# Dilated 3x3 convolution on one core: 960 one-element memsets on GpSimd, thirty in each of 32 groups

## The chip, the cores and the metric

The kernel runs on one core of one Trainium2 chip. The metric is the device time of one execution in microseconds. Most executions of a kernel agree within 0.3%. Engine names are those of the profile: PE is TensorE (PEld its weight loads), DVE is VectorE, ACT is ScalarE, POOL is GpSimd, SP is SyncE. A "q" behind a name (SPq, POOLq) is the engine's sequencer.

## The reference

Sixteen images of 64 channels and 64 x 64 pixels are convolved with 128 filters of 3 x 3, with dilation 2 and padding 2, in float32:

```python
batch, c_in, h, w, c_out, k, dilation = 16, 64, 64, 64, 128, 3, 2
...
x_pad = np.pad(x, ((0, 0), (0, 0), (pad, pad), (pad, pad)), mode='constant')
...
output[b, co] += weight[co, ci, kh, kw] * x_pad[b, ci, kh*dilation:kh*dilation+h, kw*dilation:kw*dilation+w]
```

Input x is 16.8 MB, the output 33.6 MB.

## The kernel before

Two images lie on the 128 partitions at once (64 channels each), so there are eight pairs. Each image has 64 rows, worked through in groups of 16 rows, four to a pair: 32 groups in all, and one loop over them.

SyncE loads the pairs as float32 (`load`, L65) and ScalarE casts them to float16 (`cast`, L74). VectorE adds rows two apart (`rowsum`, L86). TensorE makes three accumulations of a group in PSUM (`product`, L172): psP from the row sums, psA and psB from the cast rows. ScalarE copies psP to p_sb in SBUF (L234), and VectorE adds it to psA and to psB into the output tile osb (L241). SyncE stores the output tiles (L186, L192). Loads and stores share SyncE's one queue, in the order in which the code issues them.

Ahead of the loop stands the preparation of the weights: they are loaded (L89), VectorE, ScalarE and GpSimd form five combinations of filter rows (L112 to L116, GpSimd those at L113 and L116), and TensorE turns them. GpSimd also fills four small constants at the start of the program and makes the identity matrix (masks.py:197 and 199). It has no part in the loop.

The schedule is written by hand: the instructions of each engine keep the order of the code. The framework adds the semaphore waits that the tiles' reads and writes ask for. After the kernel's last instruction all engines meet in a closing exchange of semaphores (L310 in the profile).

The tile pools: wpool holds what lives for the whole kernel (weights, identity); the others rotate buffers.

Of the kernel before, what the change touches and what calls it, by code (L numbers as in the profile page):

```python
# [10 lines left out]
def kernel(  # L11
# [7 lines left out]
    nc = tc.nc  # L19
# [9 lines left out]
    P = 128  # L29
    f32 = mybir.dt.float32  # L30
# [14 lines left out]
    wpool = ctx.enter_context(tc.tile_pool(name="wpool", bufs=1))  # L45
# [15 lines left out]
    def load(pb, cuts=(0, H)):  # L61
        if pb not in x32_tiles:
            x32_tiles[pb] = fpool.tile([P, HW], f32, tag="x32", name="x32")
        for lo, hi in zip(cuts[:-1], cuts[1:]):
            nc.sync.dma_start(  # L65
                out=x32_tiles[pb][:, lo * W : hi * W], in_=x_pair[pb, :, lo * W : hi * W]
            )
# [10 lines left out]
    def rowsum(c):  # L78
        pb, g = divmod(c, NG)
        if g == 0:  # L80
            xs_tiles[pb] = sxpool.tile([P, HW // 2], f16, tag="xs", name="xs")
        v = x16_tiles[pb][:, g * GR * W : (g + 1) * GR * W].rearrange(
            "p (b e q) -> p b e q", e=2, q=2 * W
        )
        s = xs_tiles[pb][:, g * NH : (g + 1) * NH].rearrange("p (b q) -> p b q", q=2 * W)
        nc.vector.tensor_tensor(out=s, in0=v[:, :, 0], in1=v[:, :, 1], op=add)  # L86
# [67 lines left out]
    def casts(G):  # L154
        for n in range(2 if G else 3):
            c = ahead[0]
            if c >= ngroups or c > G + (7 if c < 2 * NG else 5):
                return
            cast(c)
            ahead[0] += 1  # L160

    def product(ps, src, kind, blk0, nblk, first, last):
        for j in (1, 0, 2):
            dw = (j - 1) * d
            o0, o1 = max(0, -dw), W - max(0, dw)
            t = kind * KW + j
            for hb in range(2):
                pp = slice(hb * CI, (hb + 1) * CI)
                rhs = src(pp, dw + o0, dw + o1)
                po = ps[:, hb * NH + blk0 * 2 * W : hb * NH + (blk0 + nblk) * 2 * W]  # L170
                po = po.rearrange("p (r w) -> p r w", w=W)[:, :, o0:o1]
                nc.tensor.matmul(  # L172
                    out=po,
                    lhsT=w_sb[pp, t * CO : (t + 1) * CO],
                    rhs=rhs,
                    start=first and j == 1,
                    stop=last and j == 2,
                )

    def blocks(x16, b0, n, e):  # L180
        v = x16.rearrange("p (b e r w) -> p b e r w", e=2, r=2, w=W)
        return lambda pp, c0, c1: v[pp, b0 : b0 + n, e, :, c0:c1]

    def store(pb, m, r0=0, r1=H, rows=((0, P),)):
        for lo, hi in rows:
            nc.sync.dma_start(  # L186
                out=out_img[2 * pb + m, lo:hi, r0 * W : r1 * W],
                in_=o_tiles[pb][lo:hi, m * HW + r0 * W : m * HW + r1 * W],
            )

    def store_both(pb, r0, r1):
        nc.sync.dma_start(  # L192
            out=out_img[2 * pb : 2 * pb + 2, :, r0 * W : r1 * W].rearrange("m o q -> o m q"),
            in_=o_tiles[pb].rearrange("p (m q) -> p m q", m=2)[:, :, r0 * W : r1 * W],
        )

    FOUR = ((0, P - 4), (P - 4, P))
    ROWS4 = 8

    for G in range(ngroups):  # L200
        pb, g = divmod(G, NG)
        x16 = x16_tiles[pb]
        xs = xs_tiles[pb].rearrange("p (r w) -> p r w", w=W)
        if g == 0:
            o_tiles[pb] = opool.tile([P, 2 * HW], f32, tag="osb", name="osb")
        o = o_tiles[pb].rearrange("p (m b e q) -> p m b e q", m=2, e=2, q=2 * W)
        b0 = g * NBLK

        def summed():
            ps = ppool.tile([P, 2 * NH], f32, tag="p", name="psP")  # L210
            sv = lambda pp, c0, c1: xs[pp, g * GR // 2 : (g + 1) * GR // 2, c0:c1]
            product(ps, sv, 0, 0, NBLK, True, True)
            return ps

        if G:
            psP = summed()

        psA = apool.tile([P, 2 * NH], f32, tag="ab", name="psA")
        product(psA, blocks(x16, b0, NBLK, 1), 1, 0, NBLK, True, False)
        z = 1 if g == 0 else 0  # L220
        product(psA, blocks(x16, b0 + z - 1, NBLK - z, 1), 2, z, NBLK - z, False, True)

        psB = apool.tile([P, 2 * NH], f32, tag="ab", name="psB")
        product(psB, blocks(x16, b0, NBLK, 0), 3, 0, NBLK, True, False)
        z = 1 if g == NG - 1 else 0
        product(psB, blocks(x16, b0 + 1, NBLK - z, 0), 4, 0, NBLK - z, False, True)

        if not G:
            psP = summed()

        if not G:
            casts(0)
        p_sb = spool.tile([P, 2 * NH], f32, tag="psb", name="p_sb")
        nc.scalar.copy(out=p_sb, in_=psP)  # L234
        if G:
            casts(G)
        if G + 1 < ngroups:
            rowsum(G + 1)
        pv = p_sb.rearrange("p (m b q) -> p m b q", m=2, q=2 * W)
        for e, ps in ((0, psA), (1, psB)):  # L240
            nc.vector.tensor_tensor(  # L241
                out=o[:, :, b0 : b0 + NBLK, e],
                in0=ps.rearrange("p (m b q) -> p m b q", m=2, q=2 * W),
                in1=pv,
                op=add,
            )

        if G == 0:
            load(XF, (0, H // 2))
        if pb == 0:  # L250
            if g % 2 == 1:
                store_both(0, (g - 1) * GR, (g + 1) * GR)
                if g == 1:
                    load(XF, (H // 2, H))
                else:
                    load(XF + 1)
        elif g == NG - 1 and pb == 1:
            store(1, 0)
            store(1, 1, 0, H // 2)
            load(XF + 2)  # L260
            store(1, 1, H // 2, H)
        elif g == NG - 1 and pb == 2:
            store(2, 0)
            load(XF + 3)
            store(2, 1)
            load(XF + 4)
        elif pb == npairs - 1:
            if g % 2 == 1:
                store(pb, 0, (g - 1) * GR, (g + 1) * GR)
                if g == 1:  # L270
                    store(pb, 1, 0, 2 * GR - ROWS4)
                    store(pb, 1, 2 * GR - ROWS4, 2 * GR, FOUR)
                else:
                    store(pb, 1, (g - 1) * GR, (g + 1) * GR)
        elif g == NG - 1:
            store(pb, 0)
            store(pb, 1)
# [37 lines left out]
```

## Time and profile before

| what | before |
|---|---|
| median of 3 runs | 126.81 us (126.58 to 126.98) |
| profiled execution, span from first to last instruction | 125.0 us |
| PE busy | 105.8 us (85%) |
| DVE busy | 91.0 us (73%), 103 instructions |
| ACT busy | 64.9 us (52%) |
| POOL busy | 2.2 us (2%), 8 instructions |
| DMA | 50.78 MB, mean 406 GB/s |

The profiled execution is told by its span alone, 125.0 us; the median of the runs is 1.8 us longer, which is what lies around the span. Busy time of an engine is the union of its instructions' recorded durations. A timeline line gives the start in us, the duration in us, the engine, the line of the code, the operation, output and input, and in brackets the engine's idle time before it with what ended it. A line "x4: 17/17/17, 124.3 to 124.9" gives a count, the shortest, median and longest duration in ns, and the first and last start in us.

### The profile page before, as it was taken

The page shows a single profiled execution, that of the slowest core. Times are in us where ns is not written, and L with a number is a line of the kernel's source. Part 1 is how long each engine was busy: PE and PEld are TensorE (multiplying, and loading weights), DVE is VectorE, ACT ScalarE, POOL GpSimd, SP SyncE. Part 2 cuts the span into 40 slices and gives each one's busy share as a digit, 9 for nine tenths or more (in the row PEclk, how much of TensorE's full clock was granted, in tenths as well). Part 3 has the DMA queues.
Part 4 walks back from the last instruction along what each step waited for, and adds up shares of the span by engine and source line. Part 5 has one row for each costly group of instructions (what it writes and reads, how often), then busy time and mean ns, then how long its engine had stood idle before and what let it go on. Part 6 is the DMA issues. An engine that isn't in the chain of part 4 may idle for free.

```text
span 125.0 us, 2343 instructions
## 1 busy us (share of the span) xinstructions
PE 105.8 (85%) x1002; PEld 57.0 (46%) x1002; DVE 91.0 (73%) x103; ACT 64.9 (52%) x68; POOL 2.2 (2%) x8
## 2 busy tenths in 40 slices
PE   6996999999999999999999999999999999600000
PEld 2353555555555555555555555555555555200000
DVE  0561998988898889888988898889888988700000
ACT  4188896665666566656665666566653333100000
POOL 2400000000000000000000000000000000000000
PEclk9999999999999999999999999999999999985555
DMA  5999999999999999999999999999999999999991
GB/s 142 368 450 435 430 401 315 430 422 420 443 427 435 412 441 438 401 435 435 425 430 427 420 435 430 435 420 435 420 430 430 430 425 435 430 414 412 420 395 73
DMA packets 4722, 50.78 MB, mean 406 GB/s; under 512 B 488, under 2 KB 488, under 8 KB 1000
## 3 DMA queue, kind: packets, MB, share of 16 engines
q1 hardware_dynamic: 4712, 50.63, 96.7%
q8 instruction: 8, 0.13, 0.4%
q14 instruction: 2, 0.02, 0.0%
HBM read 17.07 MB, written 33.55 MB: 405 GB/s over the span
## 4 chain that ended last, share of the span: by engine, by line
PE 76%; DMA 6%; ACT 2%; DVE 1%; DVEq 1%; SPq 1%; issue 0%
PE psA L172 31%; PE psB L172 30%; PE psP L172 16%; DMA x<-in_x_dram 6%; ACT x L74 2%; DVE osb L241 1%; DVEq L310 1%; ACT p_sb L234 1%; SPq L65 0%; SPq L89 0%; DVEq L241 0%
## 5 line engine op out<-in xcount | busy, mean ns | idle before, releaser
L172 PEld LDWEIGHTS <-w_sb 64*128 64x128 f16 x960 | 54.6, 94 | 45.8 <-issue 1.4
L234 ACT COPY p_sb<-psP 128x1024 f32<-128x1024 f32 x32 | 32.4, 1012 | 36.9 <-issue 21.5
L241 DVE TENSOR_TENSOR osb<-psA,p_sb 128x1024 f32<-128x1024 f32 x32 | 39.2, 1225 | 13.4 <-PE psA L172 9.8
L172 PE MATMUL psA<-x,w_sb 64*128 64x496 f16 (+3 forms) x384 | 45.1, 365 | 0.0
L172 PE MATMUL psB<-x,w_sb 64*128 64x496 f16 (+3 forms) x384 | 45.1, 365 | 0.0
L241 DVE TENSOR_TENSOR osb<-psB,p_sb 128x1024 f32<-128x1024 f32 x32 | 39.1, 1222 | 0.0
L74 ACT CAST x<-x 128x1024 f16<-128x1024 f32 (+2 forms) x31 | 32.1, 1044 | 0.5 <-DMA x<-in_x_dram 0.3
L172 PE MATMUL psP<-xs,w_sb 64*128 64x496 f16 (+1 forms) x192 | 26.0, 371 | 1.1 <-ACT p_sb L234 1.1
L86 DVE TENSOR_TENSOR xs<-x 128x512 f16<-128x512 f16 x32 | 13.3, 416 | 0.4 <-ACT x L74 0.4
L102 PE MATMUL dm<-zero 128*128 128x512 f16 x12 | 5.3, 579 | 1.2 <-DVE zero L94 1.2
L102 PEld LDWEIGHTS <-zero 128*128 128x128 f16 x12 | 1.4, 128 | 3.2 <-issue 1.8
L112 DVE CAST wd<-w 128x192 f16<-128x192 f32 x1 | 0.5, 503 | 2.4 <-DMA w<-in_weight_dram 2.4
L125 PEld LDWEIGHTS <-wd 128*64 128x64 f16 x30 | 1.0, 118 | 1.8 <-DVE wd L112 0.8
L137 ACT CAST w_sb<-wt 128x384 f16<-128x384 f32 x1 | 0.5, 478 | 2.3 <-PE wt L125 2.3
L114 ACT ACT_TABLE_LOAD x1 | 1.3, 1283 | 0.7 <-PEq L296 0.7
L125 PE MATMUL wt<-ident,wd 128*64 128x128 f16 x30 | 1.6, 241 | 0.0
L114 ACT CAST wd<-w 128x192 f16<-128x192 f32 x1 | 0.5, 539 | 1.5 <-DMA w<-in_weight_dram 1.5
L139 DVE CAST w_sb<-wt 128x384 f16<-128x384 f32 x1 | 0.6, 557 | 0.7 <-PE wt L125 0.7
L135 DVE CAST w_sb<-wt 128x384 f16<-128x384 f32 x1 | 0.6, 558 | 0.5 <-PE wt L125 0.5
L94 DVE MEMSET zero<- 128x256 uint32 x1 | 0.3, 272 | 0.9 <-PEq L296 0.9
L113 POOL TENSOR_TENSOR wd<-w 128x192 f16<-128x192 f32 x1 | 0.8, 799 | 2.3 <-DMA w<-in_weight_dram 2.3
L116 POOL CAST wd<-w 128x192 f16<-128x192 f32 x1 | 0.8, 806 | 0.0
(11 smaller groups left out, 3.8 us busy)
## 6 DMA issues: line engine op xcount, KB each, us to landing
out_dram<-osb SPq DMA_DIRECT2D x13, 2048.0 KB, 14.9
x<-in_x_dram SPq DMA_DIRECT2D x6, 2048.0 KB, 17.0
out_dram<-osb SPq DMA_DIRECT2D x5, 1024.0 KB, 13.1
x<-in_x_dram SPq DMA_DIRECT2D x2, 1024.0 KB, 13.2
x<-in_x_dram SPq DMA_DIRECT2D x1, 1088.0 KB, 5.6
x<-in_x_dram SPq DMA_DIRECT2D x1, 960.0 KB, 7.4
out_dram<-osb SPq DMA_DIRECT2D x1, 768.0 KB, 15.4
w<-in_weight_dram SPq DMA_DIRECT2D x1, 288.0 KB, 2.8
```

Source lines behind the costliest of these rows:

```text
L74: nc.scalar.copy(out=x16_tiles[pb][:, lo * W : hi * W], in_=x32_tiles[pb][:, lo * W : hi * W])
L86: nc.vector.tensor_tensor(out=s, in0=v[:, :, 0], in1=v[:, :, 1], op=add)
L102: nc.tensor.matmul(out=dm[:, 0:512], lhsT=zero[:, 0:P], rhs=zero)
L113: nc.gpsimd.tensor_tensor(out=wdv[:, 3], in0=wv[:, 0], in1=wv[:, 1], op=sub)
L114: nc.scalar.copy(out=wdv[:, 2], in_=wv[:, 0])
L116: nc.gpsimd.tensor_copy(out=wdv[:, 4], in_=wv[:, 2])
L125: nc.tensor.matmul(out=wts[k % 3][r * CI : (r + 1) * CI, c0 + j * CO : c0 + (j + 1) * CO], lhsT=wd[:, t * CI : (t + 1) * CI], rhs=ident,)
L135: nc.vector.tensor_copy(out=t0[0], in_=t0[1])
L172: nc.tensor.matmul(out=po, lhsT=w_sb[pp, t * CO : (t + 1) * CO], rhs=rhs, start=first and j == 1, stop=last and j == 2,)
L234: nc.scalar.copy(out=p_sb, in_=psP)
L241: nc.vector.tensor_tensor(out=o[:, :, b0 : b0 + NBLK, e], in0=ps.rearrange("p (m b q) -> p m b q", m=2, q=2 * W), in1=pv, op=add,)
L310: with _tile.TileContext(nc) as tc:
```

## The change

A tile of one float32 on each partition is taken from the pool of lasting tiles, and in each of the 32 groups, behind VectorE's two additions and ahead of the group's loads and stores, GpSimd is given thirty memsets of the tile's first partition, one element each. No instruction reads the tile.

```diff
@@ -194,6 +194,8 @@
+    tick = wpool.tile([P, 1], f32, name="tick")
+
     FOUR = ((0, P - 4), (P - 4, P))
     ROWS4 = 8
@@ -245,6 +247,8 @@
                 op=add,
             )
 
+        for _ in range(30):
+            nc.gpsimd.memset(tick[0:1], 0.0)
         if G == 0:
             load(XF, (0, H // 2))
         if pb == 0:
```

## The prediction

> **What bounds the kernel now.** I read the page's busy row and its forty slices, then the stretches, then GpSimd's own timeline, and last the program's closing line. The slices:
>
> ```profile
> PE   6996999999999999999999999999999999600000
> ...
> DMA  5999999999999999999999999999999999999991
> ```
>
> TensorE stops after about 108 us, but the DMA row stays at 9 to the last slice but one. The stretches (us, then busy time and count of PE, PEld, DVE, ACT, POOL, then granted clock, DMA share, GB/s) show the same with numbers:
>
> ```profile
> 36.00:67.00 31.00, 31.00 (x304) 17.02 (x300) 27.37 (x31) 19.64 (x21) 0.00 (x0) 1.00 1.00 425
> 108.00:124.00 16.00, 0.11 (x2) 0.00 (x0) 1.46 (x2) 0.00 (x0) 0.00 (x0) 0.61 0.89 373
> ```
>
> The DMA share is 1.00 while TensorE works, and 16 us of stores are still to drain after the last matmul. So the 50.78 MB set the end: the compute engines run ahead of the queue, and the chain that names TensorE for 76% of the span ends in the output drain. GpSimd is idle, 0.00 us busy, in every stretch after 5.2 us. All that it does is this:
>
> ```profile
> 0.24 0.10 POOL L296 MEMSET const-float32-0.0<- 128x1 f32 x1 [0.24 <-issue]
> 0.27 0.10 POOL L296 MEMSET const-float32-1.0<- 128x1 f32 x1
> 0.31 0.10 POOL L296 MEMSET const-bfloat16-1.0<- 128x1 bf16 x1
> 0.34 0.10 POOL L296 MEMSET const-uint8-127<- 128x1 uint8 x1
> 0.73 0.20 POOL masks.py:197 MEMSET ident<- 128x128 f16 x1 [0.29 <-POOLq L296]
> 1.01 0.29 POOL masks.py:199 TENSOR_SCALAR_AFFINE_SELECT ident<-ident 128x128 f16<-128x128 f16 x1
> 3.59 0.80 POOL L113 TENSOR_TENSOR wd<-w 128x192 f16<-128x192 f32 x1 [2.29 <-DMA w<-in_weight_dram]
> 4.33 0.81 POOL L116 CAST wd<-w 128x192 f16<-128x192 f32 x1
> ```
>
> Its last result, the cast, is done at 4.33 + 0.81 = 5.14 us. After that it only stands in the program's closing exchange of semaphores (first and last start in us):
>
> ```profile
> L310 POOLq EVENT_SEMAPHORE  x4: 17/17/17, 124.3 to 124.9; - x4
> L310 SPq DRAIN  x3: 7/7/7, 124.2 to 124.5; - x3
> ```
>
> GpSimd gathers the other engines there, at 124.3 us, and the span ends at 125.0. Whoever comes last to that exchange sets the end; today it is SyncE, with the last store landed.
>
> **The change, part by part.** Nothing is removed. The order of instructions on TensorE, VectorE, ScalarE and SyncE is the same in both programs; only buffer numbers and line numbers differ. GpSimd gets 960 memsets between its cast (L116) and the closing line. Nothing of another engine stands in their waits, so the place in the groups' loop holds nothing back: GpSimd runs through all 960 from 5.14 us on.
>
> What the words of the change hide is in the built program. All 960 memsets write the same element of the one tile tick, and from the second on each carries a wait on GpSimd's own completion semaphore, one count higher each time: memset k may start only when memset k-1 has finished writing. The four const memsets above carry no such wait, and start 0.10 / 3 = 33 ns apart although each takes 99 to 102 ns. At that pace the 960 would cost 32 us and be over at 37. With the waits they cannot overlap, and the period is the memset's own time plus the way from its end to the start of the next. A period p puts GpSimd's end at 5.14 + 960 p; it arrives at the closing exchange after SyncE if p is over (124.3 - 5.14) / 960 = 124 ns. This 124 ns decides the case.
>
> - Own time: 99 ns, from the const f32 memsets (128 partitions by one element). A memset of a single partition is nowhere in the trace; these are the nearest rows, and I take their time for it. The 128-element ident memset at 204 ns fits a fixed part near 98 plus 0.83 ns an element.
> - Gap after it: the one instruction on GpSimd that waits for GpSimd's own semaphore is the affine select at masks.py:199, which waits for the ident memset. It starts at 1.01, the memset ends at 0.73 + 0.204 = 0.934: 76 ns. That is the upper bound from rows, since a configuration instruction stands between the two in the program, and since the select must read, where a memset need not. The lower bound is the tightest wait elsewhere: p_sb is ready at 10.93 + 1.01 = 11.94 and VectorE's L241 starts at 11.97, 30 ns. A gap of nothing, or a negative one (a gain), is excluded by what the wait says: the count must rise before the next may begin.
>
> So p is between 99 + 30 = 129 and 99 + 76 = 175 ns, and both lie over 124. I put two thirds of the weight on the row of the same engine, the same semaphore and the same kind of predecessor: 129 + 2/3 x 46 = 160 ns. That GpSimd is slow to act on a wait is seen at the weights too: on the same landing VectorE and ScalarE start at 3.54 and GpSimd at 3.59.
>
> The sum: 960 x 0.160 = 153.6 us, from 5.14 on, so the memsets end at 158.7. Behind the last one stand a drain and the closing exchange, from 124.3 to 125.0 in the trace, 0.7 us, with 0.1 us for the drain: the span becomes 159.5. The profiled span of before is 125.0 and the median of its runs 126.81, so 1.8 us lie around the span: 161.3 us. With 129 ns it is 5.14 + 123.8 + 0.8 + 1.8 = 131.5, with 175 ns 5.14 + 168.0 + 2.6 = 175.7. Of the 960, the first 745 (119.2 / 0.160) lie beside the stores and cost nothing; the other 215 stick out past the end.
>
> Two small parts more. Instructions have to be fetched: the page's queue q8 shows 8 packets and 0.13 MB, 16 KB each. For the 2343 instructions of the trace that is 0.13 MB / 2343 = 55 bytes each, so 960 more are an estimated 0.053 MB, 0.1% of 50.78 MB, or 0.13 us of a saturated DMA. The 34 us by which the memsets outlast the stores cover it; without that cover, in the first rival below, it costs those 0.13 us. And VectorE shares the SBUF with GpSimd: its busy time is 91.0 of 125.0, and it waits 9.8 us for TensorE at L241, so small delays fall into slack, and larger ones are below the memsets' end as well.
>
> **The rivals.** First, hidden after all, not slower: the wait is resolved while the write of the one before is still on its way to memory (the 99 ns of a record may be mostly the acknowledgement, and the next memset's start may lie inside it), and the period is under 124 ns. For it: the const memsets have three in flight at once, 33 ns apart; L116 starts at 4.33, 0.05 before L113 has ended. Against it: in neither does the later one wait for the earlier one's count, and where one does (the select) the gap is 76 ns after the end, not before it. At 33 ns GpSimd ends at 5.14 + 31.7 = 36.8 us and the time is that of before, 126.8, or 126.9 with the fetches. It decides at 124 ns: below it the change is free, above it each further ns costs 0.96 us. I give it 0.09. The Trainium skill, "Perfetto Trace Analysis", section "GPSIMD Engine Instruction", calls the recorded span of a GpSimd instruction unreliable and wants start-to-start spacing used instead; by its rule, with the const rows' 33 ns, the memsets would be free. The trace bears that out only for instructions that do not wait.
>
> Second, VectorE and GpSimd exclude each other at the SBUF, and a memset has to stand back while a VectorE instruction runs. For it: nothing in the trace, where GpSimd works beside VectorE only at 3.59 to 5.14 (L115 with L113, 0.78 beside 0.80 us). Against it: that pair ran side by side from 3.96. The price: VectorE is busy for about 88 us between 5.2 and 109, in which the memsets would stand still: 161.3 + 88 = 249 us, or much less if only L86 (13.3 us in all) excludes them, 175 us. Whole exclusion gets 0.03; the small form lies within the range.
>
> Third, the round trip is longer than the select shows, for instance because one wait after another empties a queue: a gap of 100 ns gives p = 199 and 5.14 + 191.0 + 2.6 = 198.7 us. For it speaks that GpSimd's own four semaphore instructions of the closing line lie up to 0.6 us apart (124.3 to 124.9) at 17 ns each; against it the 76 ns of the one row that shows such a wait. I give 0.08.
>
> **How the numbers follow.** The forecast (period between 129 and 181 ns, serial) has 0.80, hidden 0.09, exclusion 0.03, a longer round trip 0.08. The predicted time is 161.3 us. The range goes from 131 (129 ns) to 181 (175 ns and 5 us for L86 or fetches in part), and leaves out the other cases with their 0.20. A measurement of this kernel can tell about 0.3% from no change, 0.4 us; faster has only 0.01 (nothing in the change shortens the stores), same has the hidden case, 0.09, slower the rest, 0.90.
>
> **What would show it.** In the profile of the changed kernel: GpSimd's row has 960 memsets and is filled until the end of the span; their start-to-start spacing is near 160 ns (between 129 and 175) while each takes about 99; DMA, TensorE and VectorE go quiet where they do now, at about 124, 108 and 109 us; the closing exchange comes right after the last memset. In the chain of waits GpSimd takes the place of the drain. It is wrong if the memsets end before 124 us or stand 33 ns apart; if the groups of L241 or L86 grow by over a few per cent, the exclusion has part in it; if the spacing changes when VectorE stops at 109, that too.

## The result: 148.8 us, and the profile after

| what | before | after |
|---|---|---|
| median | 126.75 us (126.58 to 126.98, 4 runs) | 148.82 us (148.74 to 148.95, 4 runs) |
| profiled execution, span | 125.0 us | 147.0 us |

The ratio is 1.173, with a 95% interval of 1.170 to 1.176. Two runs of the experiments below, 132.42 us of the kernel with two chains and 128.96 us of before, were over 1.5% above the fastest of their kernel and are left out of the medians. The slices of the profile after (its span is longer, so a slice is 3.7 us here and was 3.1):

```profile
PE   6997999999999999999999999999940000000000
...
POOL 1766666666666666666666666666666666666664
...
DMA  5999999999999999999999999999999993000000
```

TensorE stops where it did, the stores some three us later (the last packet of a store ends at 126.7 us, and at 123.8 before), and GpSimd goes on alone for about 20 us. The chain that ended last has gone over to it:

```profile
POOL 66%; issue 31%; DMA 2%; POOLq 0%
POOL tick L251 65%; DMA w<-in_weight_dram 2%; POOL wd L113 1%; POOL wd L116 1%; POOLq L314 0%
```

"issue" is here time between two memsets. This view counts a memset as about 100 ns and 47 ns as "issue"; the records themselves have 89 and 58. GpSimd's timeline, and the group of the memsets (busy us and mean ns of one, then GpSimd's idle us ahead of them):

```profile
5.20 141.07 POOL L251 MEMSET tick<- 1x1 f32 x960
```

```profile
L251 POOL MEMSET tick<- 1x1 f32 x960 | 85.8, 89 | 55.3
```

From 5.20 us on the 960 take 141.07, 147 ns a step: 89 ns of their own and 58 ns between. The stretches (columns as in the prediction) show that the pace is nearly the same while VectorE, TensorE and the DMA work as when all have stopped:

```profile
36.00:67.00 31.00, 31.00 (x302) 17.07 (x300) 27.37 (x31) 19.65 (x21) 18.80 (x212) 1.00 1.01 425
67.00:98.00 31.00, 31.00 (x306) 17.21 (x302) 27.33 (x31) 18.16 (x19) 18.83 (x212) 1.00 1.00 426
124.00:147.00 23.00, 0.00 (x0) 0.00 (x0) 0.00 (x0) 0.00 (x0) 13.53 (x152) 0.50 0.01 5
```

212 memsets in 31 us is 146 ns a step; in the last stretch it is 152 in the 22.3 us up to the last memset's end, 147 ns. VectorE's 27.37 us and TensorE's 31.00 are those of before, and so are VectorE's groups over the whole span (the additions of L241, here L243, take 39.2 and 39.1 us, those of L86 13.3). The closing exchange follows at once:

```profile
L314 POOLq EVENT_SEMAPHORE  x4: 17/17/17, 146.4 to 146.9; - x4
```

### The profile page after: what moved, and what is told of

Its sections match the earlier page's. It is cut to its first block, busy times and chain, and to the rows that moved or that the text cites. A ratio compares the mean times of both kernels' runs of the same rounds, so it can differ in the third digit from the quotient of the medians.

```text
span 147.0 us, 3303 instructions
## 1 busy us (share of the span) xinstructions
PE 105.9 (72%) x1002; PEld 56.9 (39%) x1002; DVE 90.7 (62%) x103; ACT 64.8 (44%) x68; POOL 88.0 (60%) x968
## 4 chain that ended last, share of the span: by engine, by line
POOL 66%; issue 31%; DMA 2%; POOLq 0%
POOL tick L251 65%; DMA w<-in_weight_dram 2%; POOL wd L113 1%; POOL wd L116 1%; POOLq L314 0%
## 5 line engine op out<-in xcount | busy, mean ns | idle before, releaser
L251 POOL MEMSET tick<- 1x1 f32 x960 | 85.8, 89 | 55.3
L243 DVE TENSOR_TENSOR osb<-psA,p_sb 128x1024 f32<-128x1024 f32 x32 | 39.2, 1224 | 13.7 <-PE psA L172 9.0
L243 DVE TENSOR_TENSOR osb<-psB,p_sb 128x1024 f32<-128x1024 f32 x32 | 39.1, 1221 | 0.0
L74 ACT CAST x<-x 128x1024 f16<-128x1024 f32 (+2 forms) x31 | 32.1, 1045 | 0.6 <-DMA x<-in_x_dram 0.6
L86 DVE TENSOR_TENSOR xs<-x 128x512 f16<-128x512 f16 x32 | 13.3, 416 | 0.4 <-ACT x L74 0.4
L113 POOL TENSOR_TENSOR wd<-w 128x192 f16<-128x192 f32 x1 | 0.8, 796 | 2.4 <-DMA w<-in_weight_dram 2.4
```

Of the source, the lines that this page charges most:

```text
L74: nc.scalar.copy(out=x16_tiles[pb][:, lo * W : hi * W], in_=x32_tiles[pb][:, lo * W : hi * W])
L113: nc.gpsimd.tensor_tensor(out=wdv[:, 3], in0=wv[:, 0], in1=wv[:, 1], op=sub)
L243: nc.vector.tensor_tensor(out=o[:, :, b0 : b0 + NBLK, e], in0=ps.rearrange("p (m b q) -> p m b q", m=2, q=2 * W), in1=pv, op=add,)
L251: nc.gpsimd.memset(tick[0:1], 0.0)
```

## The experiments

Eleven kernels, each an edit of the changed kernel. The median of before that was measured with them was 126.82 us for the first four (no wait, two chains, 15 and 27 a group) and 126.92 for the last three; the four between, with a before of 127.14 beside them, are compared with the changed kernel, 148.82. Two of these four, the memsets of 128 elements and the copies, were run once; their differences, 102 and 91 us, are far over any spread seen here.

**The wait taken away.** Each memset gets an element of its own:

```diff
-    tick = wpool.tile([P, 1], f32, name="tick")
+    tick = wpool.tile([P, 960], f32, name="tick")
...
-        for _ in range(30):
-            nc.gpsimd.memset(tick[0:1], 0.0)
+        for i in range(30):
+            nc.gpsimd.memset(tick[0:1, G * 30 + i : G * 30 + i + 1], 0.0)
```

> The 960 memsets write 960 different elements of a wider tile, so none of them waits. Theory (each memset waits for the completion of the one before, 147 ns a step): without the wait the steps fall to the const memsets' 33 ns, GpSimd is done at 5.2 + 31.7 = 37 us, and the time is that of before, 126.8 us. Rival (a memset on GpSimd costs 147 ns in throughput, waited for or not): 148.8 us again.

131.48 us, ratio 1.036 (1.030 to 1.042). The mechanism is as the theory has it, the time is not. The median step is 34 ns and GpSimd is done at 43.5 us, with 80 us to spare:

```profile
L251 POOL MEMSET tick<- 1x1 f32 x960 | 32.3, 91 | 6.0 <-issue 6.0
```

But 4.7 us were left that neither theory had. They are taken up below.

**The same waits, two chains.** The memsets write two tiles in turn:

```diff
+    tock = wpool.tile([P, 1], f32, name="tock")
...
-        for _ in range(30):
-            nc.gpsimd.memset(tick[0:1], 0.0)
+        for i in range(30):
+            nc.gpsimd.memset((tick, tock)[i % 2][0:1], 0.0)
```

> The memsets write two tiles in turn, so each waits for the last but one; the number of instructions and of waits stays the same (two waits fewer). Theory (what costs is the way from a completion to the start of what waits for it): two steps are in flight at once, the mean step falls to about half, 74 ns, GpSimd is done at 5.2 + 70.6 = 76 us, and the time is 126.8. Rival (an instruction with a wait costs 147 ns whatever it waits for): 148.8.

The mean step is 73.7 ns, half of 147, and GpSimd is done at 76.0 us. So a waiting instruction as such is not dear: the latency from a completion to the dependent start is. The time is 130.89 us (130.40 to 131.78, 3 runs; ratio 1.031, 1.024 to 1.038), again some 4 over the expected.

**Fewer memsets, still in one chain.** `range(15)` and `range(27)` in place of `range(30)`:

> Fifteen memsets in each group, 480 in all. Theory (only what outlasts the stores counts): GpSimd is done at 5.2 + 480 x 0.147 = 75.8 us, the time is 126.8. Rival (each memset disturbs the other engines or the stores by 22 us / 960 = 23 ns): 137.8.

> 27 memsets in each group, 864 in all. Theory: the end follows GpSimd with a slope of 147 ns a memset, 5.2 + 864 x 0.147 + 0.8 + 1.8 = 134.8 us (96 x 0.147 = 14.1 less than with 960). Rival (a cost in proportion to the number, 23 ns each): 126.8 + 0.9 x 22 = 146.6.

With 27 it is 134.70 us, as expected to 0.1 us: where GpSimd ends last, each memset costs its 147 ns. With 15 GpSimd is done at 75.7 us, yet the time is 129.85 (128.47 to 130.23; ratio 1.023, 1.017 to 1.029), between the two expectations: hidden memsets are not free.

**The size of the own time.** Memsets on all 128 partitions (`memset(tick, 0.0)`), and memsets of 128 elements on one partition (`[P, 128]` in the tile):

> Each memset writes one element on all 128 partitions instead of one. Theory (the own time that I took from the const rows, 99 ns, belongs to 128 partitions, and 89 to one): own time 99 to 104, the gap stays 58, a step is 157 to 162, the time 148.8 + 960 x 0.010 to 0.015 = 158 to 163 us. Rival (the number of partitions plays no part, and the const rows were longer for another reason): 148.8.

> Each memset writes 128 elements of one partition. Theory (a step is the memset's own time and a fixed gap): the own time grows by the 105 ns by which the ident memset exceeds the const ones (204 - 99), a step is 147 + 105 = 252 ns, the time 148.8 + 960 x 0.105 = 249.6 us. Rival (the step is a fixed round trip in which the own time is hidden): 148.8, or less than 200.

The first takes 158.40 us, 9.6 more: 99 ns of its own and a step of 157. The second takes 251.04: 196 ns of its own and a step of 253. Here are their groups; the idle time, divided by 960, is the gap:

```profile
L251 POOL MEMSET tick<- 128x1 f32 x960 | 95.4, 99 | 55.3
L251 POOL MEMSET tick<- 1x128 f32 x960 | 188.0, 196 | 55.1
```

Own times of 89, 99 and 196 ns leave gaps of 58, 58 and 57: the step is the own time plus a fixed gap.

**The gap of an instruction that reads.**

```diff
     tick = wpool.tile([P, 1], f32, name="tick")
+    nc.gpsimd.memset(tick, 0.0)
...
-            nc.gpsimd.memset(tick[0:1], 0.0)
+            nc.gpsimd.tensor_copy(out=tick[0:1], in_=tick[0:1])
```

> The 960 memsets are replaced by 960 copies of the element onto itself on GpSimd, each waiting for the one before. Theory (the gap of 76 ns at the affine select was longer than the memsets' 58 because the select reads): the gap is 70 to 80 ns and a step at least 165 ns, the time over 166 us. Rival (the configuration instruction ahead of the select made its gap longer): the gap is 58 as with the memsets.

239.36 us: the step's median is 236 ns, but 175 of it are the copy's own, and the gap is 61.

```profile
L252 POOL COPY tick<-tick 1x1 f32<-1x1 f32 x960 | 173.3, 181 | 58.4
```

The time is over 166 us for another reason than the theory's: a copy takes 175 ns where a memset takes 89. So the theory fell: reading lengthens the gap by 3 ns and not by 18, and the 76 ns at the affine select have another cause, which stays open. The configuration instruction ahead of it is a candidate, argued and not shown. The trace of before has two of them, 11 ns each, the last over at 0.92 us, so before the memset that the select waits for (0.94).

**VectorE and GpSimd.** In the changed kernel one memset in 960 took 421 ns (shortest, median and longest in ns). It began at 7.25 us, beside a cast on VectorE:

```profile
L251 POOL MEMSET tick<- x960: 88/89/421, 5.2 to 146.2; 1x1 f32 x192
7.16 0.48 DVE L144 CAST x<-x 128x640 f16<-128x640 f32 x1
```

Its end, 7.67, is just behind that cast's, 7.64. The experiment puts such a cast into every group:

```diff
+    cin = wpool.tile([P, 640], f32, name="cin")
+    cout = wpool.tile([P, 640], f16, name="cout")
+    nc.vector.memset(cin, 0.0)
...
+        nc.vector.tensor_copy(out=cout, in_=cin)
         for _ in range(30):
```

> VectorE gets one more cast in each group, 128x640 float32 to float16 within SBUF, the form of L144 (0.48 us), beside which one memset of the changed kernel took 421 ns instead of 89. Theory (GpSimd's write is held while that form of VectorE instruction runs): in each of the 32 groups a step is longer by some 0.3 us, up to 0.45, the memsets end 32 x 0.3 = 10 us later, the time is 158 us (156 to 163). Rival (the one long memset came from something else, such as the loading of instructions): all steps stay at 147 and the time is 148.8.

159.13 us, 10.3 more than the changed kernel, 0.32 a cast. 33 steps are long, one for each of the 32 casts and one for L144, and the memsets' longest is 451 ns; the casts themselves keep their time:

```profile
L255 POOL MEMSET tick<- x960: 88/89/451, 5.3 to 156.7; 1x1 f32 x192
```

```profile
L253 DVE CAST cout<-cin x32: 479/481/491, 14.8 to 109.9; 128x640 f16<-128x640 f32 x32
```

The Trainium skill, "SBUF — State Buffer", section "Who interferes with whom", says that a VectorE cast within SBUF can take the pair of interfaces that it shares with GpSimd, for the whole instruction, and that an addition with two inputs in SBUF is in the way only of a GpSimd instruction that reads. The runs agree with both halves: the writing memsets pass beside L86 unhindered, no longer than 90 ns, while in the experiment before this one each of the 32 additions of L86 has a copy beside it that took 259 to 448 ns in place of 175.

**Where the hidden memsets' 3.0 and 4.7 us went.** In the kernel without waits a single stream of stores works on at the end. The stretches of that kernel (the DMA share is the last but one number):

```profile
124.00:126.00 2.00, 0.00 (x0) 0.00 (x0) 0.00 (x0) 0.00 (x0) 0.00 (x0) 0.50 0.07 29
126.00:128.00 2.00, 0.00 (x0) 0.00 (x0) 0.00 (x0) 0.00 (x0) 0.00 (x0) 0.50 0.07 29
```

0.07 is about one DMA engine of sixteen. Before, the share is 0.00 from 124 us on:

```profile
124.00:126.00 2.00, 0.00 (x0) 0.00 (x0) 0.00 (x0) 0.00 (x0) 0.00 (x0) 0.50 0.00 0
```

And of the two queues that the page calls "instruction", by which the engines' instructions are brought in, q14 has grown from two packets to ten, of 8 KB each; q8 keeps its eight. Before:

```profile
q14 instruction: 2, 0.02, 0.0%
```

Without waits:

```profile
q14 instruction: 10, 0.08, 0.2%
```

Three kernels vary the number of instructions and what they write: 60 and 8 unwaited memsets a group (the tile widened to match), and five large ones (`[P, 512]`, `range(5)`, `memset(tick, 0.0)`).

> Sixty memsets in each group, 1920 in all, none waiting; GpSimd is done long before the stores. It tests where the 3.0 us of the 480 and the 4.6 us of the 960 hidden memsets went. Theory (each 8 KB packet that loads GpSimd's instructions is put into the stream of one DMA engine, all of them into the same one, and that engine's share of the stores ends later; 8 more packets made 4.6 us): 16 more packets, 126.8 + 9.2 = 136 us (134 to 138), and at the end a single DMA engine works on for about 9 us. Rival (a fixed cost of GpSimd being awake, whatever the number): 131.5.

> Eight memsets in each group, 256 in all, none waiting. Theory (packets): 2 more packets, 126.8 + 2 x 0.58 = 128.0 us (127.4 to 128.6). Rival (fixed cost): 131.5.

> Five memsets in each group, 160 in all, of 128x512 float32 each, each waiting for the one before: few instructions that write 42 MB into SBUF, with GpSimd busy to about 99 us. Theory (instruction packets): at most 2 more packets, 126.8 to 128. Rival (the memsets' writes hinder the DMA's way into or out of SBUF): more than the 131.5 of the 960 small ones, since GpSimd writes nearly without pause.

| kernel | instructions added | instruction packets added | time over before, us |
|---|---|---|---|
| five large memsets a group | 160 | 1 | 0.05 (ratio 1.0007, 0.998 to 1.004) |
| 8 a group, no wait | 256 | 2 | 1.84 (ratio 1.014, 1.007 to 1.021) |
| 15 a group, one chain | 480 | 4 | 3.03 |
| 30 a group, two chains | 960 | 8 | 4.07 |
| 30 a group, no wait | 960 | 8 | 4.66 |
| 60 a group, no wait | 1920 | 15 | 9.57 (ratio 1.072, 1.064 to 1.080) |

The large memsets write 42 MB into SBUF with GpSimd busy for 84.3 us, and cost nothing that can be measured:

```profile
L251 POOL MEMSET tick<- 128x512 f32 x160 | 84.3, 527 | 9.1
```

So it is neither the writes nor GpSimd's being awake. From two packets on, the time follows their number, at 0.5 to 0.9 us each (one kernel's runs differ by up to 1.8 us; 8 a group came out 0.16 us over the expected range). Packets and instructions grow together in this table, so it alone cannot say which of them costs. Why so much for 8 KB? The trace's list of packets says it. On an engine under load a packet begins 3 to 4 ns before the last one's recorded end. A fetch takes 309 ns (in the kernel without waits two of the eight took 427 and 646), as does a data packet of its size. But the data packet that begins right at its end is stretched: in that kernel 398 to 626 ns where 309 is usual, and 821 to 946, once 1112, where 611 is. So a fetch takes 309 ns and mostly 190 to 340 more, and it takes them from one engine, not from sixteen. That all of them fall on the same engine fits the single engine at work at the end, whose lag is about their sum: the eight fetches took 2.93 us and the packets behind them 2.05 more than usual, 4.98 in all, and the last packet ends at 128.6 us, 4.7 after the 123.8 of before. With 8 a group the sum is 1.17 us and the lag 1.26. The records do not name the engines, so this is inferred. With 60 a group there are 15 packets more, not 16, and the tail is longer, but only part of the cost. The stretch from 120 to 124 us of before, then two of this kernel:

```profile
120.00:124.00 4.00, 0.00 (x0) 0.00 (x0) 0.00 (x0) 0.00 (x0) 0.00 (x0) 0.50 0.53 225
```

```profile
120.00:124.00 4.00, 0.00 (x0) 0.00 (x0) 0.00 (x0) 0.00 (x0) 0.00 (x0) 0.50 0.93 382
127.00:133.00 6.00, 0.00 (x0) 0.00 (x0) 0.00 (x0) 0.00 (x0) 0.00 (x0) 0.50 0.06 26
```

From 127 to 133 us one engine works. But from 120 to 124 the share is still 0.93, where it was 0.53 before: the stores as a whole are some 3 us late. The late engine carries loads too, and VectorE's L243 waits 4.2 us once for a cast at L74 in this kernel. That one leads to the other was not tried.

## Why the prediction was right, step by step

- **The order on GpSimd, and that the memsets form a chain**: right. Without the chain the step is 34 ns, with two chains 73.7, with one 147.
- **The threshold and the sum**: right. 5.20 + 141.07 is 146.27, 0.7 behind it make the span of 147.0, and 1.8 around it 148.8. The kernel with 27 a group lies on the same line. GpSimd started 0.06 us later than reckoned, and from there cost what its own steps cost. (The "period between 129 and 181 ns" is a slip: 181 is the range's end in us, and the bound of the period is 175.)
- **The size of a step**: 160 ns predicted, 147 measured, inside the bounds of 129 and 175. This is the term that was mis-sized, and 960 x 13 ns are the 12.5 us between 161.3 and 148.8. Ten of the thirteen are the own time: the 99 ns belong to the const rows' 128 partitions, and one partition takes 89; "I take their time for it" was wrong by that. The other three are the gap, 58 in place of 61: that two thirds of the weight on the select came so close is luck, since no row gave the two thirds and the gap is not the select's 76 in any of the runs.
- **VectorE and GpSimd in each other's way**: right that it costs the change next to nothing, one memset and 0.33 us. But it exists: the form of L144 holds a memset, and L86 holds a GpSimd instruction that reads. The prediction held against it that L113 and L115 lay side by side in the trace; that shows little, for the held memset's record lies beside the cast just so.
- **The fetches**: wrong, and covered. "0.13 us of a saturated DMA" spread the bytes over sixteen engines, and it was read from q8, which does not grow, where q14 does. The sum has no error from it, since GpSimd outlasts the stores by 20 us. But the first rival's price, 126.9, is wrong with it: where the memsets are hidden, 960 cost 4 to 4.7 us.
- **"DMA, TensorE and VectorE go quiet where they do now"**: right for TensorE and VectorE; the stores ended later, the DMA share being 0.11 from 124 to 126 us in the profile after, against 0.00.
- **The rivals**: the period under 124 ns is seen only without the waits or in two chains; standing still beside every VectorE instruction, and a longer round trip than the select's, are seen nowhere.

## What to carry to other kernels

An instruction on an engine that is otherwise idle has two prices. If it waits for its predecessor, even one that writes the same unread element, it runs at latency: count own time plus gap (here 89 + 58 ns), times the number, and compare with the time until the kernel's end. And its own loading is a transfer: where DMA sets the end, count the packets (here one for 128 memsets), and charge each to one engine, not to sixteen (here 0.5 to 0.9 us each).

## What was not expected of the hardware

- Loading 8 KB of instructions under a saturated DMA costs some 0.6 us at the end of the kernel (4.66 us for eight packets), about twice the 0.309 us of the packet itself. The Trainium skill, "Runtime: NRT & Kernel Launch", section "Instruction fetch mechanics", calls the cost of crossing from one 16 KiB block of instructions to the next mostly hidden. In this kernel, bound by DMA, the runs show otherwise: it was hidden where GpSimd ended last, and too small to see with the one packet of the large memsets.
- A GpSimd memset of one element takes 89 ns on one partition and 99 on 128; the gap from its completion to the start of the memset that waits for it is 57 to 58 ns, with little spread.
- GpSimd's unwaited memsets seem to run out of instructions: with 34 ns a memset, the kernel without waits stood still seven times, 0.26 to 1.71 us each, 128 memsets apart, and went on 1.5 to 1.8 us after the start of a packet of q14. In the changed kernel, at 147 ns a memset, there is no such stop.
